# Sliding-window attention on merged 128-column score blocks, token-wise head sums, and a reordered conformer end in a two-layer hybrid trunk

## The chip, the cores and the metric

The kernel runs on one core of a Trainium2 chip. The time is the device time of one execution in microseconds. Three runs of the kernel before gave 1294.02, 1295.35 and 1297.88 us, median 1295.35.

## The reference

One sequence of 512 tokens, width 1024, float32. Layer 0 is a mixer: one input projection feeds a Mamba-2 head group (16 heads of 64) and a sliding-window attention (16 query heads, 2 key heads of 64, window 128, one sink logit per head); both results go through one output projection. Layer 1 is a causal conformer convolution of 31 taps. Each is followed by a gated MLP of width 2816.

```python
# attention: blocks of 128 queries, keys of the previous and the own block
logits = jnp.einsum("bnqkgd,bnskd->bnkgqs", qb, kb).astype(f32) * (dh ** -0.5)
dist = qi + blk - sj
in_window = (dist >= 0) & (dist < ATTN_WINDOW)
logits = jnp.where(valid[None, :, None, None], logits + bias, -jnp.inf)
m = jnp.maximum(jnp.max(logits, axis=-1, keepdims=True), sink)
p = jnp.exp(logits - m)
denom = jnp.sum(p, axis=-1, keepdims=True) + jnp.exp(sink - m)
out = jnp.einsum("bnkgqs,bnskd->bnqkgd", (p / denom).astype(vb.dtype), vb)
# Mamba-2 group: gated RMS norm over 2 groups of 512 channels
yf = y.astype(f32) * jax.nn.silu(z.astype(f32))
yg = yg * lax.rsqrt(jnp.mean(yg * yg, axis=-1, keepdims=True) + RMS_EPS)
# conformer
u = h @ pw1_w + pw1_b
u = u[..., :CONV_CH] * jax.nn.sigmoid(u[..., CONV_CH:])
u = causal_depthwise_conv(u, dw_w, dw_b)
u = jax.nn.silu(layer_norm(u, ln_w, ln_b))
return u @ pw2_w + pw2_b
```

Of the 256 keys that a block of queries is given, query i sees keys i+1 to 127 of the previous block and keys 0 to i of its own: always 128.

## The kernel before

Channels lie on the 128 partitions and the 512 tokens on the free axis. Every dense projection is a `gemm` (L130): weights arrive as 512 KB tiles on SP's queue, ACT rounds each to `wh` (L119), DVE takes the rest `wl` (L120), and TensorE runs three matmuls for each of 8 slices of 128 input channels (L135 to L137), 24 of 128x512 for a tile. PSUM has banks of four tags: `mm` three, `pa` two, `pb` two, `pc` one.

In the mixer no order is written out: the framework orders each engine's instructions beforehand by priority and by when their inputs should be there, so independent work is woven together. Stages follow each other as in-projection tiles and the Mamba steps (31 to 181 us), attention (182 to 278 us) and output projections (from 280 us). The gate `z` is 8 in-projection tiles of 24 matmuls each; they depend on nothing of attention and lie beside it. Each is scaled (`cv`, L221), goes through a tanh on ACT and two DVE operations (L718, L719).

`ssd_outputs` (L509) broadcasts a decay to 128 partitions with a matmul (`pair_bcast`, L269) and takes its exponential. `head_sums` (L533) sums the squares of each head: DVE splits the squares into two parts (L537, L539) and two 128x512 matmuls with a 0/1 matrix (L542) add them; ACT then copies the sums (L585) and four transposes (L588) put tokens on partitions, where the chain for the query and key norms begins (L593).

Attention goes over 32 units: head pair j (heads j and j+8), block c. `attn_logits` computes 128x256 scores for each head (L650, L651), adds the bias table and takes the row maximum in one DVE instruction (L657, with a second that reads the accumulator), the exponential on ACT (L660), the reciprocal on DVE (L663), the scaling on POOL (L665). `attn_values`, three units later, transposes the probabilities (L681), copies them out of PSUM on ACT or, for even blocks, on DVE (L686), and multiplies with the values (L690). After the fourth block the result is split in two parts (L694, L696).

Each of the 8 output tiles is one PSUM bank with two halves: attention's channels (`yb`), then Mamba's (`ya`). Five tiles open with their first halves. The group norm needs, for each of the two groups, a sum over channels (`tok_sum`, L157), a short DVE chain of 4-column operations that ends in `gr` (L736), and a broadcast (L163).

The conformer's order is written out in the program. Sixteen projection tiles give `u`; for each j a gated u goes to DRAM and back, shifted, into `u4[j]` (three buffers), and `conv_pe` runs 24 matmuls with diagonal weights on it (L884; for j = 7, 32 of them in each half of the tokens, the second half in two parts). The tail takes the layer norm's sums with 8 small matmuls per half (L941), computes its moments on DVE, broadcasts them (L958), and runs `normalise`, `residue` and `outputs` (L983 to L985) for half 0 and then half 1.

## Time and profile before

| | |
|---|---|
| median of three runs | 1295.35 us |
| profiled execution | 1297.84 us, its span 1296.0 us |
| TensorE busy | 1281.3 us (99%) |
| its weight loads | 1032.4 us (80%) |
| VectorE busy | 854.4 us (66%) |
| ScalarE busy | 515.2 us (40%) |
| GpSimd busy | 124.2 us (10%) |

The profiled execution was 2.5 us above the median of the runs. Its matmuls are pipelined: two 128x512 matmuls start 0.23 us apart, though each is shown as some 0.4 us long, so a busy share of 99% hides stretches in which the engine is not at its pace. Distances between starts tell more than busy times. On DVE, too, a following instruction starts a little before the one ahead is shown to end, so the sum of busy times exceeds the time that the instructions take in a row.

### The profile page before, as it was taken

How to read it: one execution, taken by the hardware profiler on the slowest of the kernel's cores; microseconds unless marked ns; L12 is line 12 of the kernel's file. 1: busy time of each engine (PE TensorE's matmuls, PEld its weight loads, DVE VectorE, ACT ScalarE, POOL GpSimd, SP SyncE). 2: the span in 40 equal slices, each digit the busy share in tenths (PEclk: the TensorE clock that was granted, in tenths of full speed). 3: DMA queues.
4: the chain of work that ended last, by engine and by line, in shares of the span. 5: the costliest groups of instructions: out<-in, count | busy, mean ns of one | idle time of the engine just before them, and what ended most of it. 6: DMA issues, size and time to landing. Idle time of an engine off the chain costs nothing.

```text
span 1296.0 us, 16832 instructions
## 1 busy us (share of the span) xinstructions
PE 1281.3 (99%) x6443; PEld 1032.4 (80%) x6443; DVE 854.4 (66%) x1444; ACT 515.2 (40%) x812; POOL 124.2 (10%) x198
## 2 busy tenths in 40 slices
PE   9999999999999999999999999999999999999998
PEld 7878877778888888888888876658888888888887
DVE  7986769985348777777332377857677777774221
ACT  6465547863234333333232222226433333332120
POOL 0031204640210000000011100000600000000000
PEclk9999999999999999999999999999999999999999
DMA  6312222212333333323333265550333333333331
GB/s 225 98 50 65 66 65 66 66 44 71 98 101 96 96 95 96 96 94 94 102 90 103 90 181 146 154 151 2 117 98 98 98 98 98 96 92 102 108 118 39
DMA packets 40113, 125.13 MB, mean 97 GB/s; under 512 B 4704, under 2 KB 5088, under 8 KB 40032
## 3 DMA queue, kind: packets, MB, share of 16 engines
q1 hardware_dynamic: 39312, 123.50, 31.2%
q8 instruction: 51, 0.84, 0.3%
q10 hardware_dynamic: 720, 0.55, 0.2%
q14 instruction: 30, 0.25, 0.1%
HBM read 119.73 MB, written 4.29 MB: 96 GB/s over the span
## 4 chain that ended last, share of the span: by engine, by line
PE 78%; DVE 2%; POOL 0%; DMA 0%; issue 0%; ACT 0%; SPq 0%; ACTq 0%; POOLq 0%
PE mm L135 23%; PE mm L137 23%; PE mm L136 23%; PE pa L884 3%; PE pc L690 1%; PE pa L136 1%; PE pa L137 1%; PE pa L135 1%; PE pb L681 1%; DMA u<-du 0%; PE pb L163 0%; PE mm L984 0%; PE mm L985 0%; PE mm L983 0%; POOL lt L665 0%
## 5 line engine op out<-in xcount | busy, mean ns | idle before, releaser
L135 PE MATMUL mm<-xr,wh 128*128 128x512 f32 x1120 | 439.1, 392 | 0.0
L137 PE MATMUL mm<-xr,wl 128*128 128x512 f32 x1120 | 437.2, 390 | 0.5 <-DVE wl L362 0.5
L136 PE MATMUL mm<-xr,wh 128*128 128x512 f32 x1120 | 437.2, 390 | 0.0
L119 ACT CAST wh<-wr 128x1024 fp32r<-128x1024 f32 (+1 forms) x178 | 184.0, 1034 | 453.6 <-PE mm L136 411.3
L120 DVE TENSOR_TENSOR wl<-wr,wh 128x1024 fp32r<-128x1024 f32 (+1 forms) x178 | 214.5, 1205 | 156.2 <-ACT wh L119 151.0
L137 PEld LDWEIGHTS mm<-xr,wl 128*128 128x128 f32 x1120 | 210.3, 188 | 44.6 <-DVE wl L362 1.0
L135 PEld LDWEIGHTS mm<-xr,wh 128*128 128x128 f32 x1120 | 210.4, 188 | 43.6 <-issue 1.4
L136 PEld LDWEIGHTS mm<-xr,wh 128*128 128x128 f32 x1120 | 210.4, 188 | 43.0 <-DVE xr L183 0.4
L221 DVE TENSOR_TENSOR cv<-mm,nrb 128x512 f32<-128x512 f32 x116 | 79.6, 689 | 94.4 <-PE mm L137 90.4
L136 PE MATMUL mm<-g,wh 128*128 128x512 f32 x360 | 140.0, 389 | 0.0
L135 PE MATMUL mm<-g,wh 128*128 128x512 f32 x352 | 136.9, 389 | 0.0
L137 PE MATMUL mm<-g,wl 128*128 128x512 f32 x352 | 136.9, 389 | 0.0
L216 DVE SCALAR_TENSOR_TENSOR ct<-cv,par_ffn,ct 128x510 f32<-128x510 f32 (+1 forms) x176 | 131.1, 748 | 3.5 <-issue 0.4
L136 PEld LDWEIGHTS mm<-g,wh 128*128 128x128 f32 x360 | 67.6, 188 | 14.1
L135 PEld LDWEIGHTS mm<-g,wh 128*128 128x128 f32 x352 | 66.1, 188 | 13.7
L137 PEld LDWEIGHTS mm<-g,wl 128*128 128x128 f32 x352 | 66.1, 188 | 13.6
L193 POOL TENSOR_TENSOR nsum<-nsum,nsq 128x512 f32<-128x512 f32 x21 | 34.3, 1631 | 427.0 <-ACT nsq L192 427.0
L213 ACT ACTIVATE ct<-cv,par_ffn 128x512 f32<-128x512 f32 x88 | 71.4, 814 | 3.2 <-DVE cv L221 3.0
L789 ACT ACTIVATE th<-ct 128x512 f32<-128x512 f32 x44 | 27.8, 632 | 84.5 <-DVE ct L216 84.5
L800 DVE TENSOR_TENSOR h<-h,mm 128x512 f32<-128x512 f32 x16 | 11.0, 687 | 56.3 <-PE mm L137 56.3
L884 PE MATMUL pa<-u,dg 128*32 128x512 f32 (+1 forms) x464 | 45.0, 535 | 1.4 <-DMA u<-du 1.4
L884 PEld LDWEIGHTS pa<-u,dg 128*32 128x32 f32 x464 | 14.5, 110 | 27.0 <-issue 21.5
(308 smaller groups left out, 1393.4 us busy)
## 6 DMA issues: line engine op xcount, KB each, us to landing
wr<-w_up SPq DMA_DIRECT2D x88, 512.0 KB, 3.5
wr<-w_in SPq DMA_DIRECT2D x29, 512.0 KB, 3.5
wr<-w_dn SPq DMA_DIRECT2D x32, 448.0 KB, 3.3
wr<-pw SPq DMA_DIRECT2D x24, 512.0 KB, 6.0
wr<-w_out SPq DMA_DIRECT2D x16, 512.0 KB, 3.6
wr<-w_dn SPq DMA_DIRECT2D x16, 512.0 KB, 3.5
u<-du SPq DMA_DIRECT2D x28, 266.0 KB, 5.0
h<-x SPq DMA_DIRECT2D x8, 256.0 KB, 5.6
```

Source lines behind the costliest of these rows:

```text
L119: S.copy(wh[:, :n], raw[:, :n])
L120: V.tensor_tensor(wl[:, :n], raw[:, :n], f32(wh[:, :n]), op=ALU.subtract)
L135: TE.matmul(bank, wh[:, c], xh, start=first and i == 0, stop=False)
L136: TE.matmul(bank, wh[:, c], xl, start=False, stop=False)
L137: end = TE.matmul(bank, wl[:, c], xh, start=False, stop=last and i == n - 1)
L193: eng.tensor_tensor(self.sum, self.sum, sq, op=ALU.add)
L213: S.activation(t, v, AF.Identity, bias=bias, scale=w(taps - 1))
L216: V.scalar_tensor_tensor(t[:, s:], v[:, : T - s], w(k), t[:, s:], op0=ALU.mult, op1=ALU.add)
L221: V.tensor_tensor(v, bank, rb, op=ALU.mult)
L681: TE.transpose(tb[:, blk(b * 2 + e)], lt[:, e, blk(b)], ident)
L789: S.activation(sg, c, AF.Silu)
L884: TE.matmul(cv[quad(c), :n], diag[j][:, g, c, :], u4[j][:, c, 4 * g + t0 : 4 * g + t0 + n], start=g == 0, stop=g == npe - 1 and j < 2)
```

## The change

**Attention.** 16 units: two head pairs (`jp`) and one block. Scores of 256 columns are computed as before. For blocks 1 to 3 a predicated copy in PSUM then writes the previous block's scores over the own block's where the own key lies behind the query (`before`, a mask of triu less the diagonal), so that 128 columns are left; block 0 uses its own 128. Bias addition, exponential, scaling and transposes go over 128 columns for each of four heads. The bias table is merged in the same way on the host. For the values, all merged probabilities are multiplied with the previous block's values, and their part on own keys (`own`, the transposed probabilities times triu, on DVE) with the difference `vstep` of the two blocks' values. The lag between logits and values is two units. The bias tables are loaded into the tiles of the residual stream `h`, all eight ahead of the Mamba steps' end, and `x` is loaded again after attention.

**Head sums and decays.** The squares are weights of fp32 matmuls with two 0/1 columns, four for each head pair, and the sums come out with tokens on partitions. The decay's exponential is taken from a bank that `ssd_states` fills anyway.

**Group norm.** `normed(g)` stands behind the first halves of output tiles 1 and 2.

**Conformer.** The gate's half is projected first. `conv_pe(4)` moves out of the loop to behind the last projection; blocks 5 and 6 run in halves of 256 tokens; the tail is in another order; `u4[7]` is loaded in two parts of the tokens, four transfers each.

```diff
...
+            ec = sbt("att", 16)
             for e in range(2):
                 hd = e * 8 + j
                 bank = bank_of("pa")
                 TE.matmul(bank, pairs[:, hd : hd + 1].to_broadcast([P, P]), rows_t, start=True, stop=True)
...
+                S.activation(ec[HALF[e], P:], bank[HALF[e], P:], AF.Exp)
...
-            xdt, ms, sm = ssd.pop(j)
+            xdt, ms, sm, ec = ssd.pop(j)
...
-            cb2 = pair_bcast("pa", j, 64)
-            ec = sbt("d", 3)
-            S.activation(ec[:, P:], cb2[:, P:], AF.Exp)
...
         def head_sums(src, n):
             sq = sbt("nsq", 1)
             S.activation(sq, src, AF.Square)
-            hi = sbt("cv", 2, T, F32R)
-            V.tensor_copy(hi, sq)
-            lo = sbt("th", 1, T, F32R)
-            V.tensor_tensor(lo, sq, f32(hi), op=ALU.subtract)
-            w = halves[:, 137:265] if n == 8 else halves[:, 9 - n : 137 - n]
-            for i, o in enumerate((hi, lo)):
-                TE.matmul(st_q, w, o, start=n == 8 and i == 0, stop=n == 7 and i == 1)
+            for c in range(NB):
+                cols = slice(c * 18 + n, c * 18 + n + 9, 8) if n < 8 else slice(c * 18 + 16, c * 18 + 18)
+                TE.matmul(st_q[:, cols], sq[:, blk(c)], halves[:, 0:9:8], start=True, stop=True)
...
-        ssum = sbt("d", 3)[0:32]
-        S.copy(ssum, st_q[0:32])
-        bank = bank_of("pb")
-        for c in range(NB):
-            TE.transpose(bank[:, c * 32 : (c + 1) * 32], ssum[:, blk(c)], ident[0:32, 0:32])
-        stv = bank[:, : NB * 32].rearrange("p (c k) -> p c k", c=NB)[:, :, 0:18]
-        rq = sbt("d", 3)[:, : NB * 18]
+        stv = st_q[:, : NB * 18].rearrange("p (c k) -> p c k", c=NB)
...
+        before = warm.bitcast(I32)
+        V.tensor_tensor(warm, triu, ident, op=ALU.subtract)
+        vstep = sbt("bc", 4)
+        V.tensor_tensor(vstep[:, P:], vtok[:, P:], vtok[:, : 3 * P], op=ALU.subtract)
...
-            bt = phase[0].tile([P, 2, 256], F32, name=nm("bt"), tag="bt", bufs=2)
+            bt = h[j].rearrange("p (e s) -> p e s", e=2)
             nc.sync.dma_start(bt, btab[j])
...
+        def attn_logits(jp, c):
+            lt = phase[0].tile([P, 4, 129], F32, name=nm("lt"), tag="a", bufs=4)
...
+            for j2 in range(2):
+                j = 2 * jp + j2
+                bt, qa, qb = head[j]
+                lg = bank_of("pa").rearrange("p (e s) -> p e s", e=2)
+                for e, (qq, kh, kl) in enumerate(((qa, kha, kla), (qb, khb, klb))):
+                    TE.matmul(lg[:, e, s0:], qq[:, blk(c)], kh[:, keys], start=True, stop=False)
+                    TE.matmul(lg[:, e, s0:], qq[:, blk(c)], kl[:, keys], start=False, stop=True)
+                if c:
+                    V.copy_predicated(lg[:, :, P:], before.unsqueeze(1).to_broadcast([P, 2, P]), lg[:, :, :P])
+                for e in range(2):
+                    i = 2 * e + j2
+                    V.tensor_tensor_reduce(out=lt[:, i, :P], in0=lg[:, e, P:], in1=bt[:, e, :P] if c else bt[:, e, P:],
+                                           op0=ALU.add, op1=ALU.min, scale=-1.0,
+                                           scalar=nsink[:, j + 8 * e : j + 8 * e + 1], accum_out=nmx[:, i : i + 1])
+                    S.activation(lt[:, i, :], lt[:, i, :], AF.Exp, bias=nmx[:, i : i + 1],
+                                 scale=-1.0, accum_out=den[:, i : i + 1])
             V.reciprocal(rec, den)
-            for e in range(2):
...
+            for i in range(4):
+                G.tensor_scalar(lt[:, i, :P], lt[:, i, :P], rec[:, i : i + 1], 0.0, op0=ALU.mult, op1=ALU.add)
...
+            for i in range(4):
+                TE.transpose(tb[:, blk(i)], lt[:, i, :P], ident)
+            whole_p = sbt("b", 4)
+            S.copy(whole_p, tb)
+            parts = [(vtok, max(c - 1, 0), whole_p)]
+            if c:
+                own = sbt("b", 4)
+                V.tensor_tensor(c16(own), c16(tb), triu.unsqueeze(1).to_broadcast([P, NB, P]), op=ALU.mult)
+                parts.append((vstep, c, own))
+            if c % 2 == 0:
+                acc[jp] = bank_of("pc")
+            yp = acc[jp]
+            o = c % 2 * 2 * P
+            for n, (v, b, p) in enumerate(parts):
...
+                    TE.matmul(yp[HALF[e], o : o + 2 * P], v[:, b * P + e * 64 : b * P + e * 64 + 64],
+                              p[:, e * 2 * P : (e + 1) * 2 * P], start=n == 0, stop=n == len(parts) - 1)
...
-                S.copy(pt[:, o0:], tb[:, o0:])
-            else:
-                V.tensor_copy(pt[:, o0:], tb[:, o0:])
...
-        units = [(j, c) for j in range(8) for c in range(NB)]
-        LAG = 3
...
+                for j2, (yh, yl) in enumerate(out_t[jp]):
+                    S.copy(two(yh), src[:, :, j2])
+                    V.tensor_tensor(two(yl), src[:, :, j2], two(f32(yh)), op=ALU.subtract)
...
+        units = [(jp, c) for jp in range(4) for c in range(NB)]
+        LAG = 2
...
+        def normed(g):
...
         for m, tag in enumerate(OPEN):
             banks[m] = bank_of(tag)
             out_half(m, 0, yb)
+            if m in (1, 2):
+                normed(m - 1)
...
-            nc.sync.dma_start(raws[i], pw1[(i % 2) * 8 + i // 2] if i < 16 else pw2[i - 16])
+            nc.sync.dma_start(raws[i], pw1[(i + 1) % 2 * 8 + i // 2] if i < 16 else pw2[i - 16])
...
+            first = H + 4 * (GROUPS_PE[j] - 1)
+            for a, b in ((0, first), (first, n)) if j == 7 else ((0, n),):
+                for s in range(4):
+                    nc.sync.dma_start(u4[j][quad(s), :, a:b],
+                                      du.rearrange("(c p) n -> p c n", c=4)[:, :, s + a : s + b])
...
+            if q in (None, 0):
+                cvp[j] = bank_of("mm" if j == 7 else "pa")
...
+                    sg = sigmoid(j, pg)
+                if 2 <= j < 6:
                     conv_pe(j - 2)
...
-            pa = project(14)
+                gate(j, pa, sg)
+            pg = project(14)
             make_diag(7)
             split_w(16)
+            sg = sigmoid(7, pg)
             taps(6, 0)
-            va = scaled(pa, norm.rb)
-            pg = project(15)
+            pa = project(15)
             split_w(17)
+            gate(7, pa, sg)
             taps(6, 1)
-            gate(7, va, pg)
-            conv_pe(5)
+            conv_pe(4)
             split_w(18)
-            add(5)
-            sums(5)
-            conv_pe(6)
+            add(4)
+            sums(4)
+            conv_pe(5, 0)
             split_w(19)
-            add(6)
-            sums(6)
-            conv_pe(7, 0, 0)
-            conv_pe(7, 0, 1)
+            add(5, 0)
+            sums(5, 0)
+            conv_pe(6, 0)
+            add(6, 0)
+            sums(6, 0)
+            conv_pe(7, 0)
             evacuate(0)
-            conv_pe(7, 1, 0)
+            silu = phase[0].tile([P, 1], F32, name="silu")
+            S.activation(silu, ones[:, 0:1], AF.Silu)
+            conv_pe(5, 1)
+            add(5, 1)
+            sums(5, 1)
             bank = tail_sums(0)
             lr = moments(bank)
-            conv_pe(7, 1, 1)
-            evacuate(1)
-            silu = phase[0].tile([P, 1], F32, name="silu")
-            S.activation(silu, ones[:, 0:1], AF.Silu)
+            conv_pe(6, 1)
+            add(6, 1)
+            sums(6, 1)
             sa = spread(lr)
-            bank = tail_sums(1)
-            obank = [bank_of(t) for t in ("mm", "mm", "mm", "pc")]
-            normalise(0, 0, sa)
-            for j in range(1, 8):
+            conv_pe(7, 1)
+            obank = [bank_of(t) for t in ("mm", "mm", "pc", "mm")]
+            for j in range(5):
+                normalise(j, 0, sa)
+                if j:
+                    residue(j - 1, 0)
+                if j == 1:
+                    evacuate(1)
+            outputs(0, 0)
+            lr = moments(tail_sums(1))
+            for j in range(5, 8):
                 normalise(j, 0, sa)
                 residue(j - 1, 0)
-                if j == 2:
-                    lr = moments(bank)
             residue(7, 0)
-            for j in range(8):
+            for j in range(1, 8):
                 outputs(j, 0)
-                if j == 4:
+                if j == 5:
                     sa = spread(lr)
             for j in range(8):
...
```

On TensorE, in the middle of attention, before (rows of L681 are transposes, of L690 values, of L650 and L651 scores; `mm` with L135 to L137 is a matmul of a z tile):

```order
L681 MATMUL pb_2630<-ctile,lt_2511 128x128 x4
L137 MATMUL mm_3098<-xr_166,wl_3102 128x512
L690 MATMUL pc_2561<-b_2563,bc_514 64x128 x2
L135 MATMUL mm_3098<-xr_179,wh_3101 128x512
L690 MATMUL pc_2561<-b_2588,bc_514 64x128 x4
L681 MATMUL pb_2659<-ctile,lt_2544 128x128 x4
L136 MATMUL mm_3098<-xr_181,wh_3101 128x512
L269 MATMUL pa_2620<-rows_t,sel_85 128x512
L650 MATMUL pa_2641<-kv_1794,c_2493 128x256
L651 MATMUL pa_2641<-kv_1796,c_2493 128x256
```

and now, at the place where blocks 1 and 2 of the last two head pairs are done (L643 and L644 are scores, L663 transposes, L677 values):

```order
L643 MATMUL pa_2424<-kv_1739,c_2300 128x256
L644 MATMUL pa_2424<-kv_1741,c_2300 128x256
L643 MATMUL pa_2424<-kv_1740,c_2301 128x256
L644 MATMUL pa_2424<-kv_1742,c_2301 128x256
L663 MATMUL pb_2439<-ctile,lt_2316 128x128
L677 MATMUL pc_2404<-b_2402,bc_1752 64x256 x2
L663 MATMUL pb_2439<-ctile,lt_2316 128x128 x3
L663 MATMUL pb_2486<-ctile,lt_2367 128x128 x4
L643 MATMUL pa_2461<-kv_1739,c_2240 128x256
L677 MATMUL pc_2404<-b_2444,bc_512 64x256 x2
```

Before, matmuls of z stand between attention's instructions all the way: the last 12 of z's 192 come behind the last L690. Now 119 rows in a row hold attention alone, and 61 of the 192 come behind the last L677.

On TensorE at the first halves of the output projections, before (L157 is the group norm's sum over channels, L163 its broadcast; the sum of group 0 stands ahead of the first half, 26 rows earlier):

```order
L136 MATMUL mm_3290<-att_2852,wh_3293 128x512
L137 MATMUL mm_3290<-att_2850,wl_3294 128x512
L135 MATMUL mm_3321<-att_2015,wh_3324 128x512
L163 MATMUL pb_3209<-ctile,gr_3187 128x128 x4
L157 MATMUL pb_3235<-ones,bc_2855 128x1 x4
L136 MATMUL mm_3321<-att_2017,wh_3324 128x512
```

and now, in the first half of output tile 2 (the sum of group 0 stands 15 matmuls earlier):

```order
L135 MATMUL mm_3029<-att_2359,wh_3032 128x512
L136 MATMUL mm_3029<-att_2360,wh_3032 128x512
L137 MATMUL mm_3029<-att_2359,wl_3033 128x512
L163 MATMUL pb_3003<-ctile,gr_2981 128x128 x4
L135 MATMUL mm_3029<-att_2361,wh_3032 128x512
L136 MATMUL mm_3029<-att_2362,wh_3032 128x512
```

The broadcast has moved from behind 25 matmuls of the first two tiles into the third and, for group 1, into the fifth; four small blocks stand where they did, 15 to 24 matmuls apart.

On TensorE behind the conformer's last projection, before (L884 is a convolution, L890 a rank-one correction, L941 the sums of the layer norm; `pa_7335` is block 5, `pa_7372` block 6, `pa_7409` and `pa_7447` the halves of block 7):

```order
L884 MATMUL pa_7335<-u_1408_7125,dg_7046 32x512 x24
L890 MATMUL pa_7335<-krows,neg 128x512
L884 MATMUL pa_7372<-u_1425_7242,dg_7163 32x512 x24
L890 MATMUL pa_7372<-krows,neg 128x512
L884 MATMUL pa_7409<-u_1440_7328,dg_7274 32x256 x32
L890 MATMUL pa_7409<-krows,neg 128x256
L884 MATMUL pa_7447<-u_1440_7328,dg_7274 32x256 x16
L941 MATMUL pb_7464<-ones,s_1287_6412 128x1
```

and now (L886, L892 and L945 are the same three; `pa_7040` is block 4, `pa_7077` block 5, `pa_7114` block 6, `mm_7145` block 7):

```order
L886 MATMUL pa_7040<-u_1272_6740,dg_6651 32x512 x24
L892 MATMUL pa_7040<-krows,neg 128x512
L886 MATMUL pa_7077<-u_1289_6857,dg_6778 32x256 x24
L892 MATMUL pa_7077<-krows,neg 128x256
L886 MATMUL pa_7114<-u_1304_6943,dg_6895 32x256 x24
L892 MATMUL pa_7114<-krows,neg 128x256
L886 MATMUL mm_7145<-u_1319_7026,dg_6975 32x256 x32
L892 MATMUL mm_7145<-krows,neg 128x256
L886 MATMUL pa_7077<-u_1289_6857,dg_6778 32x256 x24
L892 MATMUL pa_7077<-krows,neg 128x256
L945 MATMUL pb_7215<-ones,s_1168_6144 128x1
L945 MATMUL pb_7215<-ones,g_7179 128x1
```

Block 4 is new at this place; the second half of block 5 stands between the first half of block 7 and the sums, and the second half of block 6 behind them.

## Rows read from the trace of the kernel before

**Rows 1.** The page's first part: busy time of the engines, their share of the span, and instructions.

```profile
PE 1281.3 (99%) x6443; PEld 1032.4 (80%) x6443; DVE 854.4 (66%) x1444; ACT 515.2 (40%) x812; POOL 124.2 (10%) x198
```

**Rows 2.** Busy time of each engine in stretches of the span (from:to in us, length, then PE, PEld, DVE, ACT and POOL with their instructions, the granted TensorE clock as a share of 2.4 GHz, the DMA engines' share, GB/s): in-projection and Mamba steps, attention, first halves of the output projections with the group norm, two pieces of these, and two of the conformer's outputs.

```profile
31.00:181.00 150.00, 148.79 (x803) 119.66 (x803) 112.52 (x216) 79.50 (x164) 28.33 (x32) 1.00 0.22 70
182.35:278.34 95.99, 93.08 (x653) 72.73 (x654) 86.05 (x272) 72.30 (x194) 45.22 (x124) 1.00 0.18 56
279.42:316.13 36.71, 34.61 (x154) 28.59 (x152) 25.24 (x53) 12.86 (x18) 4.02 (x3) 0.91 0.22 72
286.00:288.00 2.00, 0.20 (x1) 0.00 (x0) 1.79 (x7) 0.83 (x1) 0.88 (x1) 1.00 0.00 0
290.00:292.00 2.00, 2.00 (x8) 1.90 (x9) 1.58 (x3) 1.14 (x3) 0.00 (x0) 0.50 0.79 236
882.00:884.00 2.00, 1.59 (x8) 1.33 (x9) 1.56 (x5) 1.78 (x4) 0.00 (x0) 0.68 0.00 0
884.00:886.00 2.00, 2.00 (x11) 2.00 (x11) 1.76 (x12) 1.09 (x2) 0.00 (x0) 0.50 0.00 0
```

**Rows 3.** Timeline of TensorE (start, length, engine, line) around one head sum and one decay broadcast.

```profile
92.23 0.50 PE L542 MATMUL mm<-th,halves 128*128 128x512 f32 x1
92.66 0.66 PE L515 MATMUL pb<-b,c 128*64 128x128 f32 x8
93.24 0.51 PE L269 MATMUL pa<-rows_t,sel 128*128 128x512 f32 x1
93.58 0.38 PE L522 MATMUL pc<-bc,d 128*128 128x128 f32 x2
```

**Rows 4.** Timeline at the start of the query and key norms.

```profile
181.13 0.58 ACT L585 COPY d<-mm 32x512 f32<-32x512 f32 x1 [1.90 <-PE mm L542]
...
182.35 0.23 DVE L593 TENSOR_TENSOR d<-pb,nr 128x72 f32<-128x72 f32 x1 [1.87 <-PE pb L588]
```

**Rows 5.** DVE in the attention stretch, grouped by line and shape (count, busy us, mean ns, idle before and what ended it).

```profile
L657 DVE CUSTOM_DVE_ANT_0 lt<-pa,bt,nsink 128x256 f32<-128x256 f32 x48 | 22.0, 478 | 2.6 <-PE pa L651 1.0 <-POOL lt L665 0.9 <-issue 0.3
L120 DVE TENSOR_TENSOR wl<-wr,wh 128x1024 fp32r<-128x1024 f32 x7 | 8.5, 1221 | 1.4 <-ACT c L637 0.7 <-ACT wh L119 0.6
...
L686 DVE COPY b<-pb 128x512 f32<-128x512 f32 x8 | 5.5, 681 | 0.2 <-PE pb L681 0.2
...
L663 DVE RECIPROCAL rec<-den 128x2 f32<-128x2 f32 x32 | 5.1, 159 | 0.6 <-ACT lt L660 0.4
L657 DVE CUSTOM_DVE_ANT_0 lt<-pa,bt,nsink 128x128 f32<-128x128 f32 x16 | 5.0, 346 | 0.3 <-POOL lt L665 0.3
L718 DVE SCALAR_TENSOR_TENSOR ct<-th,cv 128x512 f32<-128x512 f32 x7 | 4.8, 683 | 1.4 <-ACT th L716 1.4
...
L686 DVE COPY b<-pb 128x256 f32<-128x256 f32 x8 | 3.3, 415 | 0.0
```

**Rows 6.** Timeline of DVE at two places of the same stretch.

```profile
264.30 0.35 DVE L657 CUSTOM_DVE_ANT_0 lt<-pa,bt,nsink 128x128 f32<-128x128 f32 x1
...
264.57 0.48 DVE L657 CUSTOM_DVE_ANT_0 lt<-pa,bt,nsink 128x256 f32<-128x256 f32 x1
...
264.97 0.48 DVE L657 CUSTOM_DVE_ANT_0 lt<-pa,bt,nsink 128x256 f32<-128x256 f32 x1
...
269.73 0.69 DVE L696 TENSOR_TENSOR att<-pc,att 128x512 fp32r<-128x512 f32 x1
270.33 0.41 DVE L686 COPY b<-pb 128x256 f32<-128x256 f32 x1
270.66 0.68 DVE L718 SCALAR_TENSOR_TENSOR ct<-th,cv 128x512 f32<-128x512 f32 x1
```

**Rows 7.** Timeline of TensorE at the end of the z tiles.

```profile
278.96 0.39 PE L136 MATMUL mm<-xr,wh 128*128 128x512 f32 x1
279.19 0.39 PE L137 MATMUL mm<-xr,wl 128*128 128x512 f32 x1
279.42 0.95 PE L157 MATMUL pb<-ones,bc 128*128 128x1 f32 x8
280.23 0.49 PE L135 MATMUL mm<-att,wh 128*128 128x512 f32 x1
```

**Rows 8.** Waits of TensorE from 181 to 317 us (us in total, times, longest).

```profile
PE pb L163 <- DVE gr L736: 2.0, 1, 2.0
```

**Rows 9.** Waits of TensorE from 855 to 912 us.

```profile
PE pa L884 <- DMA u<-du: 1.4, 1, 1.4
PE mm L984 <- DVE g L976: 0.7, 1, 0.7
PE pb L958 <- DVE lr L152: 0.6, 1, 0.6
```

**Rows 10.** Timeline of TensorE in the conformer's tail: block 7's first half, the first output matmul and the thirteenth after it.

```profile
869.07 3.66 PE L884 MATMUL pa<-u,dg 128*32 128x256 f32 x64 [1.40 <-DMA u<-du]
...
882.85 0.58 PE L983 MATMUL mm<-dg,wh 128*128 128x256 f32 x1 [0.41 <-ACT dg L973]
...
886.04 0.33 PE L984 MATMUL mm<-g,wh 128*128 128x256 f32 x1
```

**Rows 11.** DMA issues on SP behind the last projection: u to DRAM, and the four shifted loads of block 7.

```profile
858.97 0.33 SPq L871 DMA_DIRECT2D du<-u  x1
861.57 1.75 SPq L873 DMA_DIRECT2D u<-du  x4
```

190 lines of the change are left out of this document (76 added, 114 removed).

## The prediction

> **What bounds the kernel now.** The page shows TensorE busy for 99% of the span [rows 1], but starts of 128x512 matmuls lie 0.23 us apart where each is shown 0.39 long [rows 7], so I go by distances between starts and by stretches [rows 2], and then by what DVE does in them. Up to 181 us TensorE has hardly a gap (148.8 of 150.0 shown busy, DVE 112.5): what TensorE is spared there counts in full. In attention both are nearly full, TensorE 93.1 and DVE 86.1 of 96.0 us. Here DVE sets the pace: at 0.23 us the z matmuls are work that TensorE can do whenever attention's operands are late, and DVE's remaining 9.9 us are idle pieces around waits. Behind attention the waits view has one long entry, 2.0 us for the group norm [rows 8], with no work on TensorE from 286 to 288 and then a granted clock of 0.50, which is 1.2 GHz [rows 2]. The conformer's tail has the same picture on a smaller scale: 1.4, 0.7 and 0.6 us of waits [rows 9], and 1.2 GHz in the first outputs [rows 2]. Both MLPs, over half of the span, are not touched.
>
> **The change part by part**, on the profiled execution (1297.84 us, 1.84 of it outside the span, 2.5 above the median of the runs).
>
> 1. *Head sums and decays, ahead of 181 us.* Eight broadcasts of the decay go; the next instruction starts 0.34 us after one [rows 3]: -2.7. Eighteen matmuls of the head sums go; one took 0.43, and an undisturbed 128x512 takes 0.23 [rows 3, 7]; I take 0.33: -6.0. In their place come 36 matmuls with a 128x128 fp32 weight and two columns. The nearest row is the sum over channels, four such with one column in 0.81 us [rows 7]: nine groups of 0.8 to 1.0, +8.1. Sum -0.6; with 0.23 or 0.43 for the old and 0.5 or 1.1 for a group of the new, -6 to +3. DVE loses its split of the squares there, but it isn't what ends this stretch. The exponentials that move to `ssd_states` lie on ACT, 79.5 of 150 us busy [rows 2].
>
> 2. *Norm chain.* ACT's copy and the transposes go; the chain began 1.2 us after the copy did [rows 4], and now begins some 0.2 after the last sum: -1.0.
>
> 3. *Attention, by DVE's distances between starts.* A score instruction of 256 columns takes 0.40, one of 128 columns 0.27 [rows 6]. Before 48 and 16, 23.8 us; now 64 of 128, 17.3: -6.5. Reciprocals, 32 to 16; I take 0.10 of the 0.16 shown [rows 5]: -1.6. Copies of probabilities, 8 of 512 columns at 0.60 (the distance behind an equally long operation) and 8 of 256 at 0.33 [rows 5, 6]: -7.5. New: 12 multiplications `own` of 512 columns from PSUM, 0.63: +7.6; `vstep` +0.45; the split of the result in 16 pieces of 256 columns for 8 of 512, of which 13 fall ahead of the last `own`: -0.3. New and not in this trace: 24 predicated copies of 256 columns from PSUM to PSUM. From below, the copy of 256 columns out of PSUM, 0.33; from above, with a third operand and the target read as well, twice that and a little, 0.75. It is nearest to the copy, and I take 0.38: +9.1 (7.9 to 18). The order also puts z's and the weights' operations elsewhere: ahead of the last `own` there are 2 fewer weight splits (1.14 each, 1.22 shown [rows 5]) and 11 fewer z operations at 0.60: -8.9. In all DVE's row up to its last `own` becomes 86.1 - 7.7 = 78.4 us.
>
>    With the 9.9 idle us kept, and a start 1.6 us sooner (parts 1 and 2), the last `own` ends at 182.35 - 1.6 + 78.4 + 9.9 = 269.0, and the last values some 0.7 later. But the price stands behind it: in this order 61 matmuls of z come after the last values and not 12, 61 x 0.23 = 13.9 us. z ends at 283.6, where it ended at 279.4 [rows 7]: +4.2. ACT and POOL, 72.3 and 45.2 of 96.0 us busy [rows 2], get shorter pieces, and cover nothing.
>
>    The bias tables go ahead of a weight on SP's queue, and x comes back behind attention; weight tiles have three buffers, and the DMA engines were busy for 0.18 of this stretch [rows 2]: 0.
>
> 4. *Group norm.* The stretch of the five first halves took 36.7 us [rows 2]. Five times 24 matmuls are 27.2; the four blocks of the norm, 0.8 each, 3.2 [rows 7]; the other 6.3 are the 2.0 us wait and the slow clock behind it. Now 15 matmuls, 3.4 us, lie between the sum and the broadcast, and 24 more before the second halves need the result. DVE's chain needs about 16 operations of 0.2 us, and may stand behind a weight split of 1.1: I keep 0.8 of wait at the first broadcast and 0.8 at the first `ya`. 27.2 + 3.2 + 1.6 = 32.0: -4.7. If nothing waits, -6.3; if the 2.0 come back with a slow clock, 0.
>
> 5. *Conformer's tail.* Block 4 moves from the loop to behind the last projection: the same instructions, 0. It covers the way of block 7 through DRAM: u was issued at 858.97, the loads at 861.57 [rows 11], and the matmuls could start at 869.07 after 1.4 us of idle [rows 9, 10]. Now the last projection ends some 5.7 us sooner, so do the loads, and blocks 4, 5 and 6 (half) lie ahead of block 7 still; the loads of the first half carry half of the bytes, in rows of half the length: -1.4. Spreading after the second half of block 6 (about 3 us of cover for the moments' DVE chain, where 16 of 32 convolutions and a correction covered it): -0.6. The outputs begin behind block 7's second half, with five normalised blocks prepared: the waits of 0.4 and 0.7 go (-1.1) [rows 9, 10], and with them the slow clock: the thirteenth matmul after the first started 3.19 us later [rows 10], at half of 0.23 each it would be 1.5: -1.7. Two more corrections: +0.2. -1.4 - 0.6 - 1.1 - 1.7 + 0.2 = -4.6; with a late load -3.1, and -5.5 for a tail in which every remaining gap closes.
>
> Sum: parts 1 and 2 are in the start of part 3, so the mixer is +4.2 - 4.7 = -0.5, and the conformer -4.6. In all -5.1: 1292.7 for the profiled execution, 1290 against the median. Measured differences under 0.3% (3.9 us) can't be told from none; the boundaries are 1291.5 and 1299.2.
>
> **The rivals.**
>
> *A: the stretch without z is starved, slower.* 119 rows of attention follow each other. A unit of these costs TensorE 16 instructions of some 0.12 us, 1.9, and DVE 4 x 0.27 + 2 x 0.38 + 0.1 + 0.6 + 0.35 and a share of the preparation, about 3.9. So TensorE is idle for half of some nine units (119 rows at about 13), in short pieces. In this trace a 2.0 us gap was followed by 1.2 GHz [rows 2]; a unit then costs TensorE 3.8, as much as DVE, and where each waits for the other in turn I add 0.5 to 1 us for each unit, 4 to 9 us, and some 4 for z's first matmuls at 0.43. From about 9 us on the gain is eaten and the kernel is slower: 1302. Against it: attention had many short waits before and kept 1.00 [rows 2]. The Trainium skill, "TensorE: Matmul & The Clock Gate", section "A second HAM failure mode: psum-queue depth-cycling", describes such a case: short idles between groups of matmuls that cycle through PSUM banks make the clock go down and up again, and the cost is paid between bursts. By that rule this rival is the forecast; the stretch before, full of z, does not test it. Dear predicated copies (0.75: +8.9) end at the same place, 1299.
>
> *B: TensorE is the bound throughout, a larger gain.* If DVE's idle pieces in attention were waits for TensorE, then 48 transposes less at 0.12 (5.6), the eight broadcasts and the head sums count in full and z's tail is no price: -0.6 - 1.0 - 5.6 - 4.7 - 4.6 = -16.5, 1279. For it: 99% [rows 1]. Against it: DVE 86 of 96 us [rows 2]. The Trainium skill, "Trainium Kernel Development and Optimization", Best Practices, says to judge by weight loads and not by matmul time; they are at 80% [rows 1], so the trace speaks against it too.
>
> *C: DVE waits less.* Units are twice as large, so each operation has more independent ones beside it, and the 9.9 us of idle shrink to 4: 1284.
>
> *D: only one end gains.* Block 7's shorter rows land no sooner, or attention's tail takes what the group norm gives: 1293 to 1297, no change.
>
> **How the numbers follow.** Forecast (with C beside it as its better side) 0.50, B 0.10, D 0.25, A 0.15. The forecast's cases lie between 1283 and 1292; B is faster, a little of the forecast and D are within 0.3%: faster 0.59, same 0.27, slower 0.14. The range leaves out the far end of B and most of A: 1280 to 1299; the likeliest case's own is 1283 to 1293.
>
> **What would show it.** In the trace after: z's last matmul at 281 to 286 us; the predicated copy 0.33 to 0.45 us from start to start; a granted clock of 1.00 in the stretch without z (under 0.8 is rival A); no wait of more than 1 us at L163; the first halves of the output projections in 31 to 33 us; in the conformer no wait for u4 at block 7, and outputs at 0.12 us from the first one on. The prediction falls if DVE is not the engine that is full in attention, or if the time of the MLPs moves.

## The result, and the profile after

The changed kernel takes 1299.23 us (median of ten runs) where the kernel before takes 1295.99: a ratio of 1.0029, interval 1.0017 to 1.0041. The forecast was 1290, from a range of 1280 to 1299. The kernel is slower by about 0.3%, just outside the range's upper end. The profiled executions took 1297.84 us before and 1299.63 now; the first lies 1.9 us above the median of its kernel and the second 0.4, so the two profiles differ by less than the medians.

The windows of the changed kernel, to be held against [rows 2]: attention from behind the last head sum to behind the last values, a part of it without z, the first halves of the output projections, and the conformer's two slices.

```profile
178.92:276.39 97.47, 88.64 (x445) 59.09 (x445) 80.75 (x273) 62.29 (x192) 31.49 (x79) 0.93 0.16 53
230.00:262.00 32.00, 26.18 (x137) 18.07 (x139) 26.33 (x104) 21.27 (x75) 12.13 (x34) 0.79 0.15 50
290.35:321.96 31.61, 31.30 (x153) 25.94 (x152) 19.08 (x47) 10.43 (x14) 1.68 (x2) 1.00 0.25 84
882.00:884.00 2.00, 2.00 (x44) 1.23 (x40) 1.56 (x5) 1.36 (x3) 0.00 (x0) 1.00 0.03 8
884.00:886.00 2.00, 2.00 (x29) 1.42 (x19) 1.93 (x6) 1.45 (x5) 0.00 (x0) 1.00 0.00 0
```

The same stretch of attention in the kernel before:

```profile
180.87:276.52 95.65, 92.75 (x654) 72.22 (x652) 84.26 (x269) 71.20 (x192) 45.22 (x124) 1.00 0.19 61
```

Two of the three gains are there. The first halves take 31.6 us with a clock of 1.00, and the conformer's slices are at 1.00 where they were at 0.68 and 0.50 (they now hold block 7's second half and the first outputs). Attention is longer by 1.8 us, 97.5 for 95.7, though it contains 122 matmuls of z and not 168. In it DVE is idle for 16.7 us, and before for 11.4. TensorE is shown busy for 88.6 us, and from 230 to 262 us the clock is 0.79. It falls and rises within that stretch:

```profile
230.00:236.00 6.00, 3.64 (x22) 2.14 (x22) 5.84 (x21) 3.93 (x14) 1.42 (x4) 0.99 0.26 91
236.00:242.00 6.00, 6.00 (x29) 4.71 (x29) 3.80 (x15) 4.17 (x17) 1.80 (x6) 0.50 0.27 87
248.00:254.00 6.00, 4.89 (x23) 3.58 (x25) 5.06 (x17) 3.17 (x11) 1.98 (x5) 0.72 0.00 0
254.00:260.00 6.00, 5.05 (x27) 3.43 (x25) 4.70 (x25) 4.54 (x19) 1.87 (x6) 0.72 0.27 87
```

TensorE's timeline shows the second loss behind it. The last values start at 274.51 and z goes on for 61 matmuls, to the first output matmul at 290.35; before, that came at 280.23 [rows 7].

```profile
274.51 1.95 PE L677 MATMUL pc<-b,bc 128*64 128x256 f32 x16
...
289.89 0.39 PE L136 MATMUL mm<-xr,wh 128*128 128x512 f32 x1
290.12 0.39 PE L137 MATMUL mm<-xr,wl 128*128 128x512 f32 x1
290.35 0.39 PE L135 MATMUL mm<-att,wh 128*128 128x512 f32 x1
```

With the marks of both timelines the whole difference can be laid out:

| from ... to | before | after | |
|---|---|---|---|
| start ... behind the last head sum | 180.9 | 178.9 | -2.0 |
| ... behind the last values | 95.7 | 97.5 | +1.8 |
| ... first output matmul (z, and before the norm's sum) | 3.7 | 14.0 | +10.2 |
| ... start of the last matmul of the five first halves | 35.7 | 31.4 | -4.3 |
| ... first norm sum of the last MLP (936.70, 938.21) | 620.8 | 616.5 | -4.3 |

The marks themselves differ by 1.5 us (the rounded rows add up to 1.4), the two spans by 1.6.

The longest waits in attention, TensorE first and then DVE (us in total, times, longest):

```profile
PE pb L663 <- POOL lt L656: 3.0, 6, 1.4
PE pc L677 <- DVE att L687: 2.4, 2, 2.0
PE pa L643 <- DVE nmx L649: 1.3, 2, 0.9
PE pa L643 <- ACT att L686: 0.6, 1, 0.6
```

```profile
DVE pa L646 <- PE pa L644: 5.6, 9, 1.5
DVE d L621 <- PE pa L264: 3.5, 4, 1.1
DVE att L687 <- ACT att L686: 2.6, 6, 0.6
DVE b L669 <- ACT b L665: 1.7, 4, 0.6
```

Before, the one long entry of TensorE lay behind attention [rows 8], and DVE stood idle for TensorE ahead of its 256-column score instructions for 1.0 us in all [rows 5]. Now DVE waits for scores (L644) and for the query broadcast (L264), and TensorE for POOL's scaling, for DVE and for ACT: each engine waits for the others in turn.

### The profile page after: what moved, and what is told of

Read it like the earlier page. It is cut to its first block, busy times and chain, and to the rows that moved or that the text cites. A ratio compares the mean times of both kernels' runs of the same rounds, so it can differ in the third digit from the quotient of the medians.

```text
span 1297.6 us, 16682 instructions
## 1 busy us (share of the span) xinstructions
PE 1281.2 (99%) x6423; PEld 1030.4 (79%) x6423; DVE 842.6 (65%) x1425; ACT 514.9 (40%) x829; POOL 109.9 (8%) x150
## 4 chain that ended last, share of the span: by engine, by line
PE 93%; DVE 3%; DMA 1%; POOL 1%; ACT 1%; issue 1%; SPq 0%; DVEq 0%; ACTq 0%
PE mm L135 26%; PE mm L137 26%; PE mm L136 26%; PE pa L886 3%; PE pc L677 1%; PE pb L663 1%; PE pb L511 1%; POOL lt L656 1%; PE pa L135 1%; PE pa L137 1%; PE pa L136 1%; PE mm L886 1%; PE mm L531 1%; PE pa L643 1%; PE pa L644 0%
## 5 line engine op out<-in xcount | busy, mean ns | idle before, releaser
L135 PE MATMUL mm<-xr,wh 128*128 128x512 f32 x1120 | 439.1, 392 | 0.0
L137 PE MATMUL mm<-xr,wl 128*128 128x512 f32 x1120 | 437.1, 390 | 0.2 <-DVE wl L357 0.2
L135 PEld LDWEIGHTS mm<-xr,wh 128*128 128x128 f32 x1120 | 210.5, 188 | 45.3 <-issue 2.2
L137 PEld LDWEIGHTS mm<-xr,wl 128*128 128x128 f32 x1120 | 210.3, 188 | 44.5 <-DVE wl L357 0.6
L221 DVE TENSOR_TENSOR cv<-mm,nrb 128x512 f32<-128x512 f32 x124 | 85.2, 690 | 96.9 <-PE mm L137 92.9
L135 PE MATMUL mm<-g,wh 128*128 128x512 f32 x352 | 136.9, 389 | 0.0
L137 PE MATMUL mm<-g,wl 128*128 128x512 f32 x352 | 136.9, 389 | 0.0
L137 PEld LDWEIGHTS mm<-g,wl 128*128 128x128 f32 x352 | 66.1, 188 | 13.8
L135 PEld LDWEIGHTS mm<-g,wh 128*128 128x128 f32 x352 | 66.1, 188 | 13.8
L886 PE MATMUL pa<-u,dg 128*32 128x512 f32 (+1 forms) x432 | 38.0, 499 | 0.6 <-DMA u<-du 0.6
L842 DVE TENSOR_TENSOR wl<-wr,wh 128x1024 fp32r<-128x1024 f32 x19 | 23.2, 1221 | 18.5 <-ACT wh L841 18.5
```

The costliest lines, as they stand in the source:

```text
L135: TE.matmul(bank, wh[:, c], xh, start=first and i == 0, stop=False)
L137: end = TE.matmul(bank, wl[:, c], xh, start=False, stop=last and i == n - 1)
L221: V.tensor_tensor(v, bank, rb, op=ALU.mult)
L842: (V if i < 20 else G).tensor_tensor(wl, raws.pop(i), f32(wh), op=ALU.subtract)
L886: TE.matmul(cv[quad(c)], diag[j][:, g, c, :], u4[j][:, c, 4 * g + t0 : 4 * g + t0 + n], start=g == 0, stop=g == npe - 1 and j < 2)
```

## The experiments

TensorE's own row in attention is compared throughout in one measure: each instruction from its start to the start of the next on the engine, added up by kind, from behind the last head sum to behind the last values. It contains the waits. "Scores" are 128 matmuls in every version; the number of transposes is in brackets, and the values are 224 matmuls in the old attention and 112 in the merged one. DVE idle is the length of that window less DVE's busy time. Each ratio below is to the kernel before, run beside that version; its medians were 1295.5 to 1297.5, so a difference of one or two us between two versions is not a sure one.

| | us (median) | scores, 128 | transposes | values | dummies | DVE idle |
|---|---|---|---|---|---|---|
| before | 1296 | 17.9 | 14.9 (112) | 15.4 | | 11.4 |
| after | 1299.2 | 25.8 | 16.7 (64) | 19.2 | | 16.7 |
| old attention | 1287.6 | 19.0 | 15.3 (112) | 16.3 | | 9.0 |
| merged alone | 1312.2 | 22.2 | 19.0 (64) | 22.0 | | 27.0 |
| z first | 1289.5 | 17.1 | 12.9 (64) | 17.7 | | 16.8 |
| three dummies | 1302.5 | 20.9 | 12.6 (64) | 18.0 | 10.7 | 17.0 |
| one dummy | 1301.6 | 24.2 | 15.4 (64) | 18.2 | 4.9 | 17.2 |
| z first, no merge | 1288.3 | 20.0 | 11.4 (64) | 17.1 | | 16.2 |
| z first, part on ACT | 1284.5 | 16.8 | 6.1 (64) | 17.7 | | 12.2 |
| after, part on ACT | 1293.7 | 22.5 | 11.4 (64) | 18.4 | | 11.6 |

**The old attention in the changed kernel.** The edit puts back the functions of attention, the bias loads and the buffers; head sums, decays, norm and conformer stay changed.

```diff
-        units = [(jp, c) for jp in range(4) for c in range(NB)]
-        LAG = 2
+        units = [(j, c) for j in range(8) for c in range(NB)]
+        LAG = 3
```

> The changed kernel with the attention of the kernel before (32 units, 256 columns, its bias loads and buffers); the other parts of the change stay. If attention's place is the only loss, the rest is what the traces show: about -2 for head sums and decays, -5 for the group norm, -5 for the conformer's end, so 1283 to 1286 us. If those gains lean on the merged attention (its operands, its order), 1290 or more.

Measured: 1287.56 us, ratio to the kernel before 0.9934 (0.9921 to 0.9948). Everything but attention is worth about 8 us, and the merged attention costs 11.7 in this kernel. The 8 us are less than the 10 to 13 expected. This order leaves 33 matmuls of z behind attention and not 12, one possible reason: one edit also moves what it doesn't touch.

**The merged attention alone in the kernel before.** The reverse edit.

> The kernel before with the merged attention alone. Here the order that the framework makes keeps matmuls of z in between nearly to the end (17 behind the last transposes and not 61), though everything that attention executes is the same. Theory 1 (the order is the loss): at or below the kernel before, 1290 to 1297 us. Theory 2 (the merged attention itself is slower, through its predicated copies, its lag of two and its waits): 1303 to 1308 us wherever z stands. Theory 3 (the clock falls in the stretch without z): like theory 1, with a granted clock of 1.00 there.

Measured: 1312.18 us, 1.0115 (1.0093 to 1.0136). That is beyond what theory 1 (1290 to 1297) and theory 2 (1303 to 1308) gave, but the run is not the test that its expectation took it for. No matmul of z stands in TensorE's row from 246.53 to 280.80; z runs up to there and goes on behind it:

```profile
246.53 0.45 PE L137 MATMUL mm<-xr,wl 128*128 128x512 f32 x1
...
280.80 0.39 PE L135 MATMUL mm<-xr,wh 128*128 128x512 f32 x1
```

```profile
246.53:280.80 34.27, 27.98 (x121) 16.87 (x121) 21.93 (x86) 19.36 (x70) 11.21 (x30) 0.70 0.12 41
```

So this order has a stretch of 34 us without z too (41 in the changed kernel, from 229.3 to 270.4), with a clock of 0.70. It doesn't tell the merged attention's own price from that of the stretch. DVE is idle for 27.0 us, half of it in waits for TensorE:

```profile
DVE pa L662 <- PE pa L660: 8.6, 7, 2.3
DVE d L637 <- PE pa L269: 4.5, 4, 2.1
DVE rec L670 <- ACT lt L668: 2.1, 2, 1.3
```

This version has a buffer less for the queries than the changed kernel (six, not seven, for lack of space), which was not tried by itself.

**z's banks emptied first.**

```diff
-            v = scaled(proj(), rb)
+            bank = proj()
+            with tc.high_priority(offset=AHEAD):
+                v = scaled(bank, rb)
```

> The changed kernel with one edit: the operation that empties a z bank (scaled, DVE) has high priority, so that the banks come free and z's matmuls stand between attention's to the end; none is left behind it. Theory 1: the 13.9 us behind attention go and attention gets little longer, 1287 to 1291 us. Theory 2: attention's own row of DVE still sets the end, later by what z takes on DVE, 1294 to 1299 us. Theory 3: clock 1.00 in the stretch, 1290 us.

Measured: 1289.53 us, 0.9951 (0.9937 to 0.9965). One DVE instruction per z tile, given a higher priority, takes 9.7 us off the changed kernel. Theory 1 (1287 to 1291) and theory 3 (1290) both gave this time, so it doesn't choose between z's place and the clock. Now z, and even 33 matmuls of the output's first halves, lie between attention's instructions, and the clock stays up:

```profile
178.80:285.90 107.10, 103.22 (x536) 70.26 (x536) 90.40 (x285) 68.92 (x201) 38.41 (x81) 1.00 0.20 63
230.00:262.00 32.00, 31.34 (x170) 20.80 (x168) 26.23 (x89) 21.53 (x68) 12.57 (x30) 1.00 0.16 50
```

DVE's idle time did not shrink (16.8 us); it has TensorE's other work beside it now.

**Dummy matmuls in the stretch without z**, three of 512 columns for a unit, then one of 256.

```diff
             tb = bank_of("pb")
+            if 4 * jp + c >= 5:
+                for _ in range(3):
+                    TE.matmul(tb, kha[:, :P], kha, start=True, stop=True)
```

> The changed kernel with three 128x512 matmuls more ahead of the transposes in units 6 to 16, whose result nothing reads: work for TensorE in the stretch without z, 33 x 0.23 = 7.6 us. Theory 3 (the clock of 1.2 GHz there is the loss): granted clock back at 1.00, attention ends 4 to 6 us sooner, 1293 to 1296 us. Theories 1 and 2: the clock may rise, but attention ends no sooner, 1299 to 1303 us.

> The changed kernel with one 128x256 matmul more ahead of the transposes in units 6 to 16, whose result nothing reads, 11 x 0.115 = 1.3 us in all; the order is that of the changed kernel, and its 61 z matmuls stay behind attention. Theory 3 (the clock of 1.2 GHz between 230 and 260 us is part of the loss): if the granted clock of that stretch rises from 0.79 to above 0.9, attention's last values come 2 to 5 us sooner and the total is 1294 to 1297 us. If the clock rises and the end does not move, the clock is not what costs: 1299 to 1301 us. If the clock stays, nothing is told.

Measured: 1302.47 us, 1.0047 (1.0029 to 1.0065), and 1301.55 us, 1.0041 (1.0028 to 1.0054).

The stretch from 230 to 262 us with three dummies:

```profile
230.00:262.00 32.00, 27.71 (x160) 17.98 (x161) 27.01 (x105) 22.22 (x78) 12.52 (x34) 0.95 0.15 50
```

and with one:

```profile
230.00:262.00 32.00, 26.56 (x146) 18.19 (x146) 26.60 (x104) 21.56 (x76) 11.87 (x34) 0.84 0.15 50
```

Both times lie where theories 1 and 2 put them. With three, scores, transposes and values together take 10.2 us less of TensorE's row and the dummies 10.7; the framework also put 11 more matmuls of z into attention, and the first output starts 0.6 us later than in the changed kernel. So the dummies bring back, in clock and shorter waits, what they cost, and nothing on top; by the medians the kernel is even 3.2 us slower (this profiled execution, 1300.12 us, is 2.4 below its median). With one dummy the order is the changed kernel's own, the clock rises to 0.84 only, under the 0.9 that the expectation asked for, and the last values end 0.4 us later. What 1.2 GHz costs by itself, with z left behind, stays open. The windows of the changed kernel bound it: from 236 to 260 us they add up to some 13 us at 1.2 GHz, so at 2.4 GHz TensorE could have saved 6 to 7 us at most, an estimate that takes it as never waiting there.

**A lag of three units**, on the version with z first (`LAG = 3` for `LAG = 2`).

> The version with z's banks emptied first (1289.5 us), with a lag of three units between scores and values instead of two. Theory W (DVE's idle time comes from scores that stand on TensorE behind transposes which wait for POOL's scaling): the waits of the predicated copies on scores, 3.7 us, and of transposes on POOL, 2.4, go to about 1 each, 1285 to 1287 us. Theory B (scores come late because only two score banks are there and each is held until DVE has read it, whatever the lag): 1289 to 1291 us.

Measured: 1291.42 us, 0.9965 (0.9952 to 0.9977), next to theory B's range. Theory W's cure fails: transposes take 15.6 us in TensorE's row, more than with a lag of two, and the two waits are 7.0 and 2.8 us where it asked for 1 each. But the longer lag hardly reached TensorE: the order is made beforehand, and in 14 of the 16 units it has as many scores ahead of the transposes as with a lag of two, mostly those of one unit more. So theory W itself is not refuted.

**Without the predicated copies**, on the version with z first.

```diff
-                if c:
-                    V.copy_predicated(lg[:, :, P:], before.unsqueeze(1).to_broadcast([P, 2, P]), lg[:, :, :P])
```

> The version with z's banks emptied first, without the 24 predicated copies: the previous block's scores are computed and not used, so attention sees the own block alone. Theory R (DVE's row of instructions sets attention's end): 24 x 0.38 = 9.1 us go from the row and the last values come 7 to 9 us sooner; the total, 1281 to 1284 us. If the copies stand in idle time of DVE: 1287 us or more.

Measured: 1288.31 us, 0.9938 (0.9924 to 0.9951). Nine us of DVE instructions gone, 1.2 us gained by the medians, and that is no sure gain: the intervals of the two versions overlap. It is the time given for copies that stand in idle time of DVE (1287 or more). DVE's row alone does not set the end. (27 matmuls of z fall behind attention again, no matmul of the first halves stands in attention, and the clock from 230 to 262 us is 0.95, so the comparison isn't of the copies alone.)

**Scaling on DVE**, one multiply of 4x128 columns for POOL's four instructions, and **half of the scaling on ACT**, both with z first:

```diff
             for i in range(4):
-                G.tensor_scalar(lt[:, i, :P], lt[:, i, :P], rec[:, i : i + 1], 0.0, op0=ALU.mult, op1=ALU.add)
+                if i % 2:
+                    S.activation(lt[:, i, :P], lt[:, i, :P], AF.Copy, scale=rec[:, i : i + 1])
+                else:
+                    G.tensor_scalar(lt[:, i, :P], lt[:, i, :P], rec[:, i : i + 1], 0.0, op0=ALU.mult, op1=ALU.add)
```

> The version with z's banks emptied first (1289.5 us), with the scaling of the probabilities on DVE, one multiply of 4x128 columns for a unit in place of four on POOL. Theory P (TensorE is the bound, and stands at transposes because POOL hands the four heads over 0.35 us apart): the transposes' share of TensorE's row, 12.9 us for 64 now, falls towards 64 x 0.12 = 7.7, and the total by about as much, 1284 to 1286 us. Theory R (DVE's row sets the end): 16 x 0.6 = 9.6 us more on DVE, 1294 to 1299 us.

> The same with two of a unit's four scalings on ACT and two left on POOL. Theory P: transposes wait half as long, 1286 to 1288 us. Theory R: DVE's row is as before, and ACT's 32 operations lie in its idle time, 1289.5 us; if ACT is late for the exponentials, more.

Measured: 1296.76 us, 1.0002 (0.9989 to 1.0015), on DVE; 1284.49 us, 0.9904 (0.9891 to 0.9917), on ACT, the fastest of all, and more than theory P asked for. In the changed kernel POOL hands over four heads in 1.42 us, and TensorE, which runs its row in order, stands at the transposes with the next scores behind them. POOL's timeline at one such place (clock 0.99 from 230 to 236 us):

```profile
234.24 1.42 POOL L656 TENSOR_SCALAR lt<-lt,rec 128x128 f32<-128x128 f32 x4 [5.64 <-DVE rec L654]
```

and TensorE's:

```profile
233.01 0.28 PE L644 MATMUL pa<-kv,c 128*128 128x256 f32 x1
234.67 1.37 PE L663 MATMUL pb<-ctile,lt 128*128 128x128 f32 x4 [1.38 <-POOL lt L656]
235.81 0.34 PE L643 MATMUL pa<-kv,c 128*128 128x128 f32 x1
```

The wait is entered with 1.38 us. The four transposes then take 1.14 us to the next start, and are shown as busy: each starts 0.06 us behind the end of its own head's scaling. With half of the scaling on ACT four of them can take 0.35 us:

```profile
242.14 0.60 PE L666 MATMUL pb<-ctile,lt 128*128 128x128 f32 x4
242.49 0.48 PE L136 MATMUL mm<-xr,wh 128*128 128x512 f32 x1
```

All 64 transposes take 6.1 us there and not 12.9. On DVE there is no room for the scaling: with the 16 multiplies it is busy for 98.7 of 108.7 us, and the time, in theory R's range, goes up by 7 us:

```profile
179.70:288.44 108.74, 100.37 (x540) 70.41 (x539) 98.72 (x300) 68.40 (x200) 8.20 (x16) 0.98 0.20 63
```

So each theory holds on one side: taking 9 us from DVE gives little, giving it as much is too much. The second half isn't DVE's share alone, for this order also has 19 us, from 254.1 to 273.5, with neither z nor first halves.

**The same help for the old attention, and for the changed kernel as it is.**

> The changed kernel with the attention of the kernel before and with z's banks emptied first. In its order 23 matmuls of z, not 33, stand behind attention. If z behind attention is the loss here too, 10 x 0.23 = 2.3 us go: 1285 us. If attention gets as much longer by z's operations on DVE: 1287 to 1288 us.

> The old attention with z's banks emptied first (1286.5 us), with one of a unit's two scalings on ACT instead of POOL. If the gain of the merged version with ACT's help (1284.5 us) came from the scaling's place alone, the old attention gains as much from it: 1281 to 1284 us. If it needs the merged blocks, because ACT has no room beside 64 exponentials of 257 or 129 columns and 16 copies of 512: 1286 us or more.

> The changed kernel, without the edit on z's banks, with two of a unit's four scalings on ACT. In its order 40 matmuls of z are behind attention, not 61. If TensorE's row sets attention's end, the transposes' share falls from 16.7 to some 8 us and the last values come 5 to 8 us sooner, and 9.1 us of z are left behind it: 1290 to 1294 us. If DVE's row sets it: the last values no sooner, 1295 to 1299 us.

Measured, in this order: 1286.53 us, 0.9926 (0.9914 to 0.9939); 1284.56 us, 0.9907 (0.9891 to 0.9923); 1293.67 us, 0.9981 (0.9969 to 0.9992). The first lies between its two cases and decides nothing. The merged attention costs 11.7 us against the old one in the changed kernel, 3.0 with z first, and nothing with z first and ACT's help: what the best version gains comes from where z and the scaling stand, and not from the merged blocks. The old attention gains 2.0 us by ACT's help, the merged one 5.0.

In the changed kernel ACT's help makes the transposes shorter by 5.3 us, the last values come 2.9 us sooner, and with 40 matmuls of z behind them and not 61 the first output starts 7.7 us sooner. The time is the one given for TensorE's row as the bound (1290 to 1294), though by smaller steps than expected (transposes at some 8 us, last values 5 to 8 sooner). DVE's busy time shows what else went:

```profile
178.75:273.50 94.75, 86.20 (x467) 57.68 (x466) 83.15 (x276) 72.70 (x226) 18.05 (x47) 0.98 0.19 60
```

DVE is idle for 11.6 us, where it was for 16.7, and for 11.4 in the kernel before: the added idle time goes when POOL hands over two heads and not four. The clock from 230 to 262 us rose with it, to 0.95, and z's order moved, so the run doesn't say how much of the gain is the clock's.

**Norm alone and conformer alone in the kernel before.**

> The kernel before with the group norm behind the first halves of output tiles 1 and 2, nothing else; attention's order stays as it was. By the prediction's own step -4.7 us, 1290.5 to 1291.5 us, no wait over 1 us at L163 and a clock of 1.00 in the first halves. If the second halves then wait for the normed operands: 1293 to 1296 us.

> The kernel before with the changed conformer alone. By the prediction's own step -4.6 us, 1290.5 to 1292 us: no wait of TensorE for the loads of block 7, and outputs at full pace from the first on. If the gain needs the shorter mixer: 1295 us.

Measured: 1292.30 us, 0.9971 (0.9959 to 0.9982), and 1291.34 us, 0.9959 (0.9947 to 0.9971). Both gains stand by themselves, the norm's somewhat smaller than expected, with a wait of 0.2 us at L163 and a clock of 1.00 in the first halves. The conformer's tail of the changed kernel shows why, with no wait of TensorE entered from 840 to 912 us:

```profile
868.34 0.38 PE L892 MATMUL pa<-krows,neg 128*128 128x256 f32 x1
868.65 3.66 PE L886 MATMUL mm<-u,dg 128*32 128x256 f32 x64
...
880.01 0.38 PE L892 MATMUL pa<-krows,neg 128*128 128x256 f32 x1
880.23 1.10 PE L962 MATMUL pb<-ctile,lr 128*128 128x128 f32 x8
881.25 3.66 PE L886 MATMUL mm<-u,dg 128*32 128x256 f32 x64
884.85 0.39 PE L892 MATMUL mm<-krows,neg 128*128 128x256 f32 x1
885.07 0.28 PE L987 MATMUL mm<-dg,wh 128*128 128x256 f32 x1
885.19 0.28 PE L988 MATMUL mm<-g,wh 128*128 128x256 f32 x1
```

Block 7 starts 0.31 us behind the correction of block 6, where it came after 1.4 us of idle [rows 10], the broadcast follows the second half of block 6 at once, and the outputs begin 0.12 us apart.

## Why the prediction was wrong

1. *Head sums and decays*, -0.6 forecast, with -1.0 for the chain. The last head sum ended 2.0 us sooner, and the chain began 3.3 us sooner, at 179.09 for 182.35 [rows 4]. Four new matmuls took 0.81 us (178.11 to 178.92), where I took 0.9. Right in sign and too small by 1.7; the rest of the difference was not split up.

2. *Attention.* This step failed, at the sentence "With the 9.9 idle us kept". DVE's instructions are as forecast: 78.4 us busy from the chain's start to the end of the last `own`, against 78.4.

```profile
179.09:273.85 94.76, 85.93 (x425) 57.59 (x425) 78.37 (x269) 61.02 (x190) 30.63 (x78) 0.93 0.17 54
```

That they meet to 0.1 us is partly luck. The predicated copy is shown with 0.42 us and took 0.34 from start to start, where I took 0.38; `own` took 0.61 for 0.63; and the 23.8 us of the old score instructions are 23.5 by the distances named there (48 x 0.40 + 16 x 0.27).

```profile
L649 DVE CUSTOM_DVE_ANT_0 lt<-pa,h,nsink 128x128 f32<-128x128 f32 x64 | 19.4, 345 | 0.9 <-PE pa L644 0.5 <-DVE rec L654 0.3
L646 DVE COPY_PREDICATED pa<-warm,pa 128x256 f32<-128x256 int32 x24 | 9.9, 424 | 5.7 <-PE pa L644 5.6
L669 DVE TENSOR_TENSOR b<-pb,ctile 128x512 f32<-128x512 f32 x12 | 8.2, 687 | 1.7 <-ACT b L665 1.7
```

But DVE was idle for 16.4 us in that row in place of 9.9. The last `own` ended at 273.9 and not at 269.0, in spite of the start 1.7 us sooner than forecast; the last values came 2.5 us behind it and not 0.7, at 276.4 in place of 269.7. These 6.7 us are nearly the whole distance from the 1292.7 forecast for the profiled execution to its 1299.6.

Two more sentences lie under that one: "Here DVE sets the pace", and that ACT and POOL "get shorter pieces, and cover nothing". POOL, busy for only 31.5 of 97.5 us, was in the way: TensorE's transposes stand behind its four scalings, the next scores behind the transposes, and DVE behind the scores. With half of the scaling on ACT, DVE's idle time in attention falls from 16.7 to 11.6 us, and with z first, where the clock from 230 to 262 us is 1.00 with and without that edit, from 16.8 to 12.2. Nine us less on DVE gave 1.2 (with z first); shorter waits of TensorE's row for POOL gave 5. What I took for a spare engine runs its row in order, and a part of its waits is shown as busy time. Rival B, TensorE as the bound, named the engine but not the sign: the 48 transposes less were worth nothing, since 64 took 16.7 us where 112 had taken 14.9.

3. *z behind attention*, 13.9 us forecast for 61 matmuls: 14.0 measured, right to 0.1 us. 9.7 us came back when z's banks were emptied first, which also drew first halves of the output into attention.

4. *Group norm*, -4.7: -4.3 from first output matmul to last, or -5.1 with the sum over channels that lay ahead of it. The wait at L163 is 0.2 us where 0.8 was kept, and the stretch took 31.6 us for 32.0. Right.

5. *Conformer*, -4.6: -4.3 over the whole way from the last first half to the last MLP. The signs named for it are all there (no wait for block 7's loads, outputs 0.12 us apart from the first on); its terms were not measured one by one.

Rival A (the stretch without z is starved) was the nearest, at 0.15: its mechanism is there, in a clock of 0.79 from 230 to 262 us and engines that wait in turn, at 1299 and not 1302. From 230 to 236 us, ahead of the first fall, TensorE is shown busy for 3.64 of 6.00 us. How much of the loss is the clock and how much the waits, the runs didn't separate. The rule named with it, of the Trainium skill, "TensorE: Matmul & The Clock Gate", section "A second HAM failure mode: psum-queue depth-cycling", agrees with this trace in that the clock went down and up in the stretch that cycles through PSUM banks, with gaps of up to 2.0 us. The ground given against rival A, that attention had kept 1.00 before, held for an attention with z in its gaps, which was the thing removed.

Against rival B stood the Trainium skill, "Trainium Kernel Development and Optimization", Best Practices, which judges the distance to the roofline (the engine's peak) by weight loads (and by the share of peak arithmetic), not by matmul time. The trace agrees: weight loads take 59.1 of 97.5 us in attention now, 61%, where TensorE is shown busy for 91%. By that measure TensorE was far from full there, and still its row held the others up.

## What to carry to other kernels

Where an order is made beforehand, read from it what fills the gaps of the engine that runs in order, and count a tail of pure work behind a stage of waits as a loss that a priority can undo; try that before judging the stage itself. TensorE, which runs its row in order, stood at the first operand that was late. A slow producer that hands over a consumer's operands one after another (here POOL with four scalings) can lengthen the consumer's row though it is itself idle most of the time, and the profile shows a part of that as busy. A stage's idle time isn't a constant that a restructured stage inherits: bound it from both sides like an unknown operation. And before a run counts as a test, read from its trace that it has the order that it was meant to have: two of these (the merged attention alone, the lag of three) did not.

## What was not expected

Four transposes of 128 columns take some 0.4 us of TensorE when their operands are there (64 in 6.1 us), and 1.14 us when POOL scales one head every 0.35. Removing 9 us of work from an engine that is busy for 84% of a stage (90.4 of 107.1 us) changed the whole by 1.2 us, and adding as much changed it by 7. The best version, 1284.5 us, is as fast with the old attention as with the merged one, which the whole change was built around. Left untried are a second bank for the values (`pc`, where TensorE waited 2.0 us once) and the clock by itself.
